# Weight splits of the output products, a first norm and clearing moved, and weights placed 64 bytes further, in a two-block transformer kernel on one core

## The chip, the cores and the metric

The kernel runs on one core of a Trainium2 chip. Its metric is the device time of one execution in microseconds (us); the figure quoted is the median of three runs. The profile comes from one profiled execution. Engines are named as the profile names them: PE is TensorE (PEld its weight loads), DVE is VectorE, ACT is ScalarE, POOL is GpSimd, SP is SyncE, which issues the weight DMAs.

## The reference

The input is 256 tokens of width 1024. A first block runs one layer: a mixer (a gated delta rule over chunks on one half of the width, a gated linear recurrence on the other) and an MLP of width 4096 with a squared ReLU. A second block puts 16 learned tokens in front (272 tokens) and runs two layers, each of a gated MLP, a mixer (stick-breaking attention and a convolution, gated and joined) and another gated MLP:

```python
def second_block(...):
    h = jnp.concatenate([meta_b, x], axis=1)
    for l in range(DEPTH_2):
        h = h + 0.5 * swiglu(rmsnorm_2(h, ffn1_norm[l]), ...)
        h = h + hybrid_mixer(rmsnorm_2(h, mix_norm[l]), ...)
        h = h + 0.5 * swiglu(rmsnorm_2(h, ffn2_norm[l]), ...)
    h = rmsnorm_2(h, final_norm)
    return h[:, N_META:]

def hybrid_mixer(u, ...):
    q, k, v, a, b, g_sb, g_conv = jnp.split(u @ w_in, IN_SPLITS, axis=-1)
    y_sb = stick_breaking_attention(q, k, v) @ w_attn_out
    y_conv = conformer_conv(a, b, ...) @ w_conv_out
    m = jax.nn.sigmoid(g_sb) * y_sb + jax.nn.sigmoid(g_conv) * y_conv
    return m @ w_out
```

All is float32, with weights of some 243 MB that are read once.

## The kernel before, in words

Activations lie transposed, with the width on 128 partitions and tokens along the free axis. A product is a **job**: one tile of 128 output columns, accumulated in one PSUM bank over 2 to 32 k-tiles of 128. Each float32 operand is held as a high part and a rest, and a k-tile costs three matmuls: high weight by high x, high weight by low x, low weight by high x (the three matmul lines of `job`, L532, L533 and L534 in the profile). Their moving operand has 256 tokens, or 272 in the second block; in that block's second layer ("layer 2" in the title, `layer == 1` in the code) the 16 learned tokens are no longer needed after the attention's keys and values, and q, the two gates gc and gs, and everything behind them have 256.

`plan` lists the jobs in order, `layout` cuts them into **units** of up to 8 k-tiles (1024 weight columns) and packs units into chunks of 2048 columns, each one DMA on SP. For every unit ScalarE copies the raw weights to a high part `wh` (the copy on L274, five buffers) and VectorE subtracts it from the raw weights to get the rest `wl` (the subtraction on L286, four buffers). `POOLED` names the kinds whose every n-th split goes to GpSimd instead (L491): every fourth of the input products, every second of ys (attention output) and o2 (mixer output), every one of yc (convolution output), some of the first block. ys and yc have 4 k-tiles, so their units have 512 columns. `emit_split` issues splits up to `LEAD` = 3 units ahead of the product in work.

The order of instructions on each engine is fixed when the program is built. Work beside the products is written as generators, **flows**, that are stepped between the k-tiles of a job whenever a planner's clock for VectorE and TensorE says that they are due. On the chip each engine then takes its instructions strictly in that order. The planner prices instructions by formulas of its own; it knows nothing of the places of operands or of two engines being in each other's way.

The flows that matter here:
- `residual` adds a finished output tile to the stream `H`, makes the next product's operand (high part on ScalarE, low part on VectorE), and adds its squares to `acc1`. In the first block's mixer and in o2 the add of squares is on GpSimd (`add=pt`), else on VectorE.
- `norm_rows` sums `acc1` over partitions by small matmuls (`tok_sums`), takes the inverse root on VectorE with a dozen tiny instructions, and spreads it over partitions by matmuls again (`to_rows`, into `R`). The products don't wait for the norm, which is applied when they are evacuated; the first MLP applies it only at its end. But the small matmuls stand in TensorE's queue.
- `do_ys` multiplies the attention's gate by the ys tile; `do_yc` multiplies the other gate by the yc tile, adds both, and splits the sum into the operand of o2. The o2 products of the first two tiles are a `pair`: k-tiles 0 to 5 of both, then 6 and 7 of both.
- `layer_norm` makes the operand of yc.
- At the start of a mixer GpSimd clears buffers for queries and values (`QZ`, `VZ`), for the attention weights (`AM`) and some borders. They lie in an arena that takes the place of the MLP's hidden activations, so clearing waits for that MLP's last product.

In the built program the operands x start 128 bytes past a multiple of 256, and the weight buffers 192 bytes past one, 4096 bytes apart; a k-tile's weights are 512 bytes, a k-tile of x 1024 or 1280. In layer 2 q, gc and gs read x from token 16 on, 64 bytes further.

Of the kernel before, what the change touches and what calls it, by code (L numbers as in the profile page):

```python
# [15 lines left out]
NM = 16  # L16
# [6 lines left out]
MIX1 = 17100  # L23
MIX2 = 16200
XW = 320
LEAD = 3
MINLEAD = 2
RAW = 3
TMPS = 9
# [3 lines left out]
POOLED = [(("a", "b", "q", "k", "v", "gc", "gs"), 4), (("ys", "o2"), 2), (("yc", ), 1), (("o1b",), 2), (("K", "Q"), 8)]  # L33
# [73 lines left out]

def layout():
# [3 lines left out]
    for j, (_, _, _, _, _, kts) in enumerate(plan()):  # L112
        mine = []
        for ks in kts:
            n = 128 * len(ks)
            limit = 1024 if len(chunks) <= 2 else CHUNK_COLS
            if not chunks or chunks[-1][1] + n > limit:
# [106 lines left out]
def tile_hybrid_blocks(  # L224
# [11 lines left out]
    jobs = plan()  # L236

# [148 lines left out]
    def tick():  # L386
# [8 lines left out]
        while st["split"] < min(st["unit"] + LEAD + 1, len(units)) and clk["V"] < clk["P"] + AHEAD:  # L395
            emit_split(st["split"])
# [64 lines left out]
    for kinds, every in POOLED:  # L461
        mine = [i for i, u in enumerate(units) if jobs[u[0]][0] in kinds]
        on_pool.update(mine[every - 1::every])

    def emit_high(u):
        while st["high"] <= min(u, len(units) - 1):
            i = st["high"]
            _, ks, c, o = units[i]
            emit_dma(c)
            n = 128 * len(ks)  # L470
            h = whp.tile([128, 1024], F32R, tag="wh", name="wh")
# [3 lines left out]
            cp(h[:, 0:n], src)  # L475
# [5 lines left out]
    def emit_split(u):  # L481
        while st["split"] <= min(u, len(units) - 1):
            i = st["split"]
            emit_high(i + (i > 0))
            _, ks, c, o = units[i]
            n = 128 * len(ks)
            lo = wlp.tile([128, 1024], F32R, tag="wl", name="wl")
            was, cur[0] = cur[0], Flow()
            cur[0].t, cur[0].eng = h_at.pop(i), "A"
            if i in on_pool:  # L490
                nc.gpsimd.tensor_tensor(out=lo[:, 0:n], in0=raw[c][:, o:o + n], in1=wh[i][:, 0:n].bitcast(F32), op=SUB)  # L491
                op("G", 0.1 + 0.00215 * n)
            else:
                tt(lo[:, 0:n], raw[c][:, o:o + n], wh[i][:, 0:n].bitcast(F32), SUB)
# [4 lines left out]
            if i + 1 < len(units) and units[i + 1][2] != c:  # L499
# [6 lines left out]
    def job(kind, x, n, o=0, bank_=None, last=True, start=None):  # L506
# [14 lines left out]
        for u in mine:  # L521
            st["unit"] = u
            emit_split(u + MINLEAD)
            h, lo = wh.pop(u), wl.pop(u)
            clk["P"] = max(clk["P"], w_at.pop(u) + LAT)
            for i, k in enumerate(units[u][1]):
# [3 lines left out]
                s = slice(128 * i, 128 * i + 128)  # L530
# [419 lines left out]
    junk = const.tile([128, 128], F32, name="junk")  # L950
    zero = const.tile([1, 512], BF16, name="zero")
# [378 lines left out]
    start_flow(norm_rows(acc1[:, 0:T1], T1, 1.0 / 1024, 1e-6, R[:, 0:T1], [ev_sq2], ev_r2))  # L1330
# [86 lines left out]

    def swiglu(x, ev_r, o, n, next_g, old_phase, final=False):
# [28 lines left out]
        for m in range(FF2):  # L1447
# [5 lines left out]
            start_flow(evac(ga, ua, m))  # L1453
        x.done()
# [12 lines left out]
    def mixer(x, ev_r, layer, next_g, old_phase):  # L1467
# [9 lines left out]
        QZ = [arena.get(4, n) for _ in range(2)]  # L1477
# [3 lines left out]
        VZ = arena.get(3, 4, 192)  # L1481
# [24 lines left out]
        def keep_q(t, b, ev):  # L1506

            for i in range(2):
                p = slice(64 * i, 64 * i + 64)
                cp(QZ[i].f[p, t], b[p, 0:n])  # L1510
# [78 lines left out]
        def values():  # L1589
            yield from wait(ev_r, *ev_v)  # L1590
            for i, (s0, sn) in enumerate(sblocks):
# [4 lines left out]
                for par in range(2):  # L1596
                    p = slice(64 * par, 64 * par + 64)
                    act(VZ.f[0:sn, i, :, 128 * par:128 * par + 64], v4(b[0:sn])[:, :, p], AF.Copy, scale=RC[0:sn, i:i + 1])
# [14 lines left out]
        def head(hp, par):  # L1613
# [7 lines left out]
            for t0, tn in blocks:  # L1621
                S = t0 + tn
                mm(b[:, col:col + S], QZ[par].f[:, hp, t0 - o:t0 - o + 128], KT.f[:, hp, 0:S])
# [51 lines left out]
            V = VZ.f[:, :, hp, 64 * par:64 * par + 128]  # L1675
# [195 lines left out]
```

## Time and profile before

| | before |
|---|---|
| median of three runs | 1520.81 us (1519.14 to 1522.02) |
| profiled execution | 1520.58 us |
| its span, first to last instruction | 1518.9 us |
| PE / DVE / ACT / POOL busy, share of the span | 97% / 71% / 53% / 13% |
| granted TensorE clock, mean | 0.990 of full speed |
| HBM read | 245.63 MB |

A busy share says how much of the span an engine worked, not that it set the end. Matmuls are pipelined: each is listed with some 0.28 us, but they start about 0.12 us apart, and the distance of their starts is what a product costs. A bracket behind a row of a timeline gives how long the engine idled before it, and what ended that.

### The profile page before, as it was taken

To read this page: it belongs to the slowest core of one execution; us is meant where nothing else is said; L and a number is where in the kernel's file an instruction comes from. 1 tells how busy PE (TensorE), PEld (TensorE's weight loads), DVE (VectorE), ACT (ScalarE), POOL (GpSimd) and SP (SyncE) were. 2 spreads that over 40 slices of the span, in tenths; PEclk is the share of its full clock that TensorE was granted. 3 is DMA by queue.
4 is the path that set the end of the run, shared out by engine and by line. 5 is a ranking of instruction groups with operands and counts; after the bars stand their busy time and mean duration, and the time that the engine had idled before them with its cause. 6 is when DMAs were issued, how large, how long until landed. Compare 5 with 4: busy or idle time off the path is not lost.

```text
span 1518.9 us, 29471 instructions
## 1 busy us (share of the span) xinstructions
PE 1478.2 (97%) x12130; PEld 1457.5 (96%) x12130; DVE 1075.8 (71%) x1882; ACT 802.7 (53%) x1365; POOL 198.3 (13%) x236
## 2 busy tenths in 40 slices
PE   7999999999999999999999999999999999999997
PEld 6889899999999999999999999999999989999997
DVE  5986866667666568998866655666568996866664
ACT  4568666544544445555644444544444655555553
POOL 3330300000000012234400000000003233500000
PEclk9999999999999999999999999999999999999999
DMA  6312455554545544433455544545454423465552
GB/s 226 142 57 84 142 194 194 193 196 143 217 167 178 177 173 143 153 123 111 162 200 171 184 169 162 203 169 181 166 182 166 167 102 122 170 219 195 188 179 79
DMA packets 36376, 248.58 MB, mean 164 GB/s; under 512 B 3984, under 2 KB 5264, under 8 KB 12304
## 3 DMA queue, kind: packets, MB, share of 16 engines
q1 hardware_dynamic: 35248, 245.50, 45.7%
q8 instruction: 95, 1.56, 0.4%
q10 hardware_dynamic: 992, 1.19, 0.2%
q14 instruction: 41, 0.34, 0.1%
HBM read 245.63 MB, written 1.05 MB: 162 GB/s over the span
## 4 chain that ended last, share of the span: by engine, by line
PE 83%; DVE 12%; ACT 3%; issue 1%; POOL 1%; DMA 0%; DVEq 0%; SPq 0%; ACTq 0%; POOLq 0%
PE bank L532 26%; PE bank L534 26%; PE bank L533 26%; PE bank L317 4%; DVE bank L297 2%; DVE wl L286 2%; DVE arena L286 2%; DVE arena L297 2%; ACT arena L274 1%; DVE arena L313 1%; PE bank L321 1%; DVE x L286 1%; ACT wh L274 1%; DVE tmp L286 0%; POOL acc L309 0%
## 5 line engine op out<-in xcount | busy, mean ns | idle before, releaser
L532 PE MATMUL bank<-x,wh 128*128 128x272 f32 (+1 forms) x2752 | 796.1, 289 | 10.8 <-ACT x L274 9.8
L534 PE MATMUL bank<-x,wl 128*128 128x272 f32 (+1 forms) x2752 | 784.1, 285 | 5.6 <-DVE wl L286 4.7
L533 PE MATMUL bank<-x,wh 128*128 128x272 f32 (+1 forms) x2752 | 785.1, 285 | 3.0 <-DVE x L286 2.3
L286 DVE TENSOR_TENSOR wl<-raw,wh 128x1024 fp32r<-128x1024 f32 (+4 forms) x453 | 532.6, 1177 | 183.4 <-PE bank L534 152.6
L274 ACT ACTIVATE wh<-raw 128x1024 fp32r<-128x1024 f32 (+4 forms) x510 | 494.5, 976 | 257.0 <-issue 136.1
L532 PEld LDWEIGHTS bank<-x,wh 128*128 128x128 f32 x2752 | 523.8, 190 | 14.4 <-ACT x L274 10.9
L533 PEld LDWEIGHTS bank<-x,wh 128*128 128x128 f32 x2752 | 523.9, 190 | 6.3 <-DVE x L286 4.4
L534 PEld LDWEIGHTS bank<-x,wl 128*128 128x128 f32 x2752 | 523.5, 190 | 6.7 <-DVE wl L286 5.6
L534 PE MATMUL bank<-hid,wl 128*128 128x272 f32 (+1 forms) x960 | 270.6, 282 | 0.0
L533 PE MATMUL bank<-hid,wh 128*128 128x272 f32 (+1 forms) x960 | 270.6, 282 | 0.0
L532 PE MATMUL bank<-hid,wh 128*128 128x272 f32 (+1 forms) x960 | 270.6, 282 | 0.0
L533 PEld LDWEIGHTS bank<-hid,wh 128*128 128x128 f32 x960 | 180.6, 188 | 0.0
L532 PEld LDWEIGHTS bank<-hid,wh 128*128 128x128 f32 x960 | 180.6, 188 | 0.0
L534 PEld LDWEIGHTS bank<-hid,wl 128*128 128x128 f32 x960 | 180.6, 188 | 0.0
L491 POOL TENSOR_TENSOR wl<-raw,wh 128x512 fp32r<-128x512 f32 (+3 forms) x57 | 107.9, 1904 | 190.1 <-PE bank L534 90.9
L286 DVE TENSOR_TENSOR tmp<-bank,R 128x272 f32<-128x272 f32 (+1 forms) x184 | 78.7, 429 | 64.8 <-PE bank L534 63.9
L274 ACT ACTIVATE tmp<-tmp 128x272 f32<-128x272 f32 (+1 forms) x140 | 59.3, 425 | 114.6 <-DVE tmp L286 78.4
L297 DVE SCALAR_TENSOR_TENSOR bank<-arena,C,bank 128x272 f32<-128x272 f32 (+1 forms) x232 | 102.2, 490 | 3.7 <-ACT bank L274 2.5
L1484 POOL MEMSET arena<- 64x1088 f32 (+1 forms) x4 | 3.9, 976 | 761.9 <-PE bank L534 761.9
L286 DVE TENSOR_TENSOR hid<-tmp,hid 128x272 fp32r<-128x272 f32 (+1 forms) x120 | 51.7, 433 | 38.3 <-ACT hid L274 38.3
L274 ACT ACTIVATE hid<-tmp 128x272 fp32r<-128x272 f32 (+1 forms) x120 | 51.0, 426 | 42.3 <-DVE tmp L286 40.7
L274 ACT ACTIVATE x<-H,C 128x272 fp32r<-128x272 f32 (+2 forms) x64 | 30.0, 486 | 81.6 <-DVE H L286 81.2
(200 smaller groups left out, 949.8 us busy)
## 6 DMA issues: line engine op xcount, KB each, us to landing
raw<-in_w_dram SPq DMA_DIRECT2D x187, 1024.0 KB, 4.8
raw<-in_w_dram SPq DMA_DIRECT2D x32, 960.0 KB, 4.7
raw<-in_w_dram SPq DMA_DIRECT2D x16, 896.0 KB, 4.6
raw<-in_w_dram SPq DMA_DIRECT2D x2, 512.0 KB, 6.0
H<-in_xt_dram SPq DMA_DIRECT2D x1, 544.0 KB, 6.6
LG<-in_lgw_dram SPq DMA_DIRECT2D x1, 512.0 KB, 6.0
out_dram<-H SPq DMA_DIRECT2D x2, 256.0 KB, 2.2
LM<-in_cm_dram SPq DMA_DIRECT2D x1, 320.0 KB, 5.2
```

The costliest lines, as they stand in the source:

```text
L274: nc.scalar.activation(out, in_, func, scale=scale, **kw)
L286: nc.vector.tensor_tensor(out=out, in0=a, in1=b, op=fn)
L297: nc.vector.scalar_tensor_tensor(out=out, in0=a, scalar=s, in1=b, op0=op0, op1=op1)
L313: nc.vector.tensor_tensor_scan(out=out, data0=a, data1=b, initial=initial, op0=op0, op1=op1)
L317: nc.tensor.matmul(out, lhsT, rhs, start=start, stop=stop)
L321: nc.tensor.transpose(out, in_, identity)
L491: nc.gpsimd.tensor_tensor(out=lo[:, 0:n], in0=raw[c][:, o:o + n], in1=wh[i][:, 0:n].bitcast(F32), op=SUB)
L532: nc.tensor.matmul(acc, h[:, s], xh, start=first and done == 0, stop=False)
L533: nc.tensor.matmul(acc, h[:, s], xl, start=False, stop=False)
L534: nc.tensor.matmul(acc, lo[:, s], xh, start=False, stop=last and done == total - 1)
L1484: nc.gpsimd.memset(QZ[i].f[64 * (1 - i):64 * (1 - i) + 64], 0.0)
```

## The change

- **Loads.** ys and yc tiles are taken in twos: two units of 512 columns are one **load**, one copy on ScalarE and one split of 1024 columns. All other units are a load each; `LEAD` and the buffers count loads. Number and order of matmuls and DMAs stay.
- **Where splits run.** ys and o2 leave `POOLED`: all their splits are on VectorE. Of yc every second load stays on GpSimd. The add of squares behind o2 moves from GpSimd to VectorE.
- **First norm.** The flow `norm_rows` in front of the first MLP starts after its fifth tile (m = 4) and no longer ahead of the first.
- **Clearing once.** `QZ` and `VZ` get a buffer of their own, cleared by GpSimd once, in the first gated MLP of the second block (at m = 8). `AM` and the borders are cleared at each mixer as before.
- **64 bytes.** `wh` and `wl` buffers grow from 1024 to 1088 columns (4352 bytes apart). For q, gc and gs of layer 2 the weights are written and read 16 columns, 64 bytes, further on. The arenas and two small tiles are moved to make room.

```diff
-MIX1 = 17100
-MIX2 = 16200
+MIX1 = 16448
+MIX2 = 11800
+SHARED = ("ys", "yc")
+WBUF = 1024 + 64
+LATE = ("q", "gc", "gs")
-POOLED = [(("a", "b", "q", "k", "v", "gc", "gs"), 4), (("ys", "o2"), 2), (("yc", ), 1), (("o1b",), 2), (("K", "Q"), 8)]
+POOLED = [(("a", "b", "q", "k", "v", "gc", "gs"), 4), (("yc",), 2), (("o1b",), 2), (("K", "Q"), 8)]
...
+    loads, load_of = [], []
+    for u, (j, ks, c, o) in enumerate(units):
+        if jobs[j][0] in SHARED and nth_of_kind(j) % 2:
+            loads[-1][2] += 128 * len(ks)
+            load_of.append((len(loads) - 1, 128 * len(ks)))
+        else:
+            loads.append([c, o, 128 * len(ks), jobs[j][0], NM * (jobs[j][2] == 1 and jobs[j][0] in LATE)])
+            load_of.append((len(loads) - 1, loads[-1][4]))
...
-            h = whp.tile([128, 1024], F32R, tag="wh", name="wh")
+            h = whp.tile([128, WBUF], F32R, tag="wh", name="wh")
...
-            cp(h[:, 0:n], src)
+            cp(h[:, a:a + n], src)
...
-                s = slice(128 * i, 128 * i + 128)
+                s = slice(o_w + 128 * i, o_w + 128 * i + 128)
...
-    start_flow(norm_rows(acc1[:, 0:T1], T1, 1.0 / 1024, 1e-6, R[:, 0:T1], [ev_sq2], ev_r2))
...
     for m in range(FF1):
         start_flow(do_ff1(pairs["ff1"].pop(0) if m < 2 and "ff1" in PAIRED else job("ff1", xb, T1), m))
+        if m == 4:
+            start_flow(norm_rows(acc1[:, 0:T1], T1, 1.0 / 1024, 1e-6, R[:, 0:T1], [ev_sq2], ev_r2))
...
+    held_pool = ctx.enter_context(tc.tile_pool(name="held", bufs=1))
+    QZ = [held_pool.tile([128, 4, T2], F32, name=f"qz{i}") for i in range(2)]
+    VZ = held_pool.tile([128, 3, 4, 192], F32, name="vz")
...
+            if m == 8 and not zeroed:
+                zeroed.append(True)
+                zeros()
...
-        for i in range(2):
-            nc.gpsimd.memset(QZ[i].f[64 * (1 - i):64 * (1 - i) + 64], 0.0)
-            nc.gpsimd.memset(AM[i].f, 0.0)
-        nc.gpsimd.memset(VZ.f, 0.0)
+        for a in AM:
+            nc.gpsimd.memset(a.f, 0.0)
...
-            start_flow(residual(b, m, nx, next_g(m), acc1[:, 0:n], ev_sq, o, add=pt))
+            start_flow(residual(b, m, nx, next_g(m), acc1[:, 0:n], ev_sq, o))
```

## Rows read from the trace of the kernel before

**Rows 1.** The page's part 1: busy us, share of the span, instructions.
```profile
PE 1478.2 (97%) x12130; PEld 1457.5 (96%) x12130; DVE 1075.8 (71%) x1882; ACT 802.7 (53%) x1365; POOL 198.3 (13%) x236
```
**Rows 2.** Windows: stretch, its length, busy us (instructions) by engine, clock, DMA.
```profile
192.00:355.00 163.00, 163.00 (x1441) 163.00 (x1440) 108.62 (x175) 93.55 (x155) 0.00 (x0) 1.00 0.53 189
376.00:553.70 177.70, 177.70 (x1443) 177.70 (x1442) 110.48 (x156) 85.15 (x117) 0.00 (x0) 1.00 0.52 182
```
**Rows 3.** PE timeline at the start of the first MLP.
```profile
178.56 0.28 PE L532 MATMUL bank<-x,wh 128*128 128x256 f32 x1
...
181.97 1.01 PE L317 MATMUL bank<-ones,acc 128*128 128x1 f32 x4 [2.58 <-POOL acc L309]
...
188.65 0.91 PE L317 MATMUL bank<-M,nr 128*128 128x128 f32 x6
...
191.98 0.28 PE L532 MATMUL bank<-x,wh 128*128 128x256 f32 x1
```
**Rows 4.** Windows: the stretch behind that wait, clock third from the end.
```profile
182.60:190.00 7.40, 7.40 (x39) 7.27 (x40) 6.46 (x20) 2.90 (x7) 0.11 (x1) 0.60 0.42 146
```
**Rows 5.** DVE timeline there: the weights of tile m = 2.
```profile
178.44 1.23 DVE L286 TENSOR_TENSOR wl<-raw,wh 128x1024 fp32r<-128x1024 f32 x1 [0.47 <-ACT wh L274]
```
**Rows 6.** Windows: the o2 pairs of both layers, and what follows in layer 2.
```profile
719.10:732.10 13.00, 11.24 (x74) 10.61 (x74) 11.10 (x18) 6.70 (x11) 6.28 (x4) 0.87 0.42 144
...
1298.70:1309.00 10.30, 8.11 (x51) 7.39 (x50) 8.08 (x17) 5.84 (x11) 3.72 (x3) 0.83 0.47 177
...
1308.40:1326.00 17.60, 17.60 (x150) 17.60 (x151) 15.72 (x19) 10.79 (x22) 12.82 (x9) 1.00 0.55 196
```
**Rows 7.** PE timeline: waits in the output products of both layers.
```profile
722.43 0.39 PE L532 MATMUL bank<-x,wh 128*128 128x272 f32 x1 [1.38 <-ACT x L274]
...
1284.17 0.39 PE L534 MATMUL bank<-x,wl 128*128 128x256 f32 x1 [0.90 <-POOL wl L491]
...
1301.93 0.38 PE L532 MATMUL bank<-x,wh 128*128 128x256 f32 x1 [1.38 <-ACT x L274]
```
**Rows 8.** DVE timeline in the output products of layer 2.
```profile
1299.56 1.86 DVE L286 TENSOR_TENSOR arena<-arena 128x256 f32<-128x256 f32 x1
...
1301.79 0.42 DVE L286 TENSOR_TENSOR arena<-arena 128x256 f32<-128x256 f32 x1
...
1308.88 2.68 DVE L286 TENSOR_TENSOR wl<-raw,wh 128x1024 fp32r<-128x1024 f32 x1 [0.65 <-ACT wh L274]
```
**Rows 9.** POOL timeline in the same stretch.
```profile
1282.84 13.74 POOL L491 TENSOR_TENSOR wl<-raw,wh 128x512 fp32r<-128x512 f32 x10 [5.30 <-PE bank L533]
1299.32 1.83 POOL L491 TENSOR_TENSOR wl<-raw,wh 128x768 fp32r<-128x768 f32 x1 [2.73 <-PE bank L534]
...
1307.85 5.99 POOL L491 TENSOR_TENSOR wl<-raw,wh 128x1024 fp32r<-128x1024 f32 x2 [2.88 <-PE bank L534]
```
**Rows 10.** PE timeline: a gs product of layer 2, two starts 24 matmuls apart.
```profile
1265.08 0.28 PE L532 MATMUL bank<-x,wh 128*128 128x256 f32 x1
...
1267.96 0.28 PE L532 MATMUL bank<-x,wh 128*128 128x256 f32 x1
```
**Rows 11.** Windows: the gate products of layer 2.
```profile
1206.00:1252.00 46.00, 44.48 (x341) 42.16 (x339) 44.89 (x92) 26.25 (x63) 14.11 (x24) 1.00 0.34 120
1252.60:1275.60 23.00, 23.00 (x181) 22.36 (x180) 16.22 (x42) 11.18 (x26) 5.11 (x5) 1.00 0.32 116
```
**Rows 12.** POOL timeline at the start of layer 2's mixer.
```profile
1141.90 0.95 POOL L1484 MEMSET arena<- 64x1024 f32 x1 [390.37 <-PE bank L534]
...
1146.58 2.39 POOL L491 TENSOR_TENSOR wl<-raw,wh 128x1024 fp32r<-128x1024 f32 x1
```
**Rows 13.** DVE timeline there.
```profile
1143.34 0.50 DVE L297 SCALAR_TENSOR_TENSOR x<-H,C,x 128x272 fp32r<-128x272 f32 x1 [0.59 <-ACT x L274]
...
1146.65 2.35 DVE L293 TENSOR_SCALAR rs_y<-RC 128x3 int32<-128x3 int32 x1
```
**Rows 14.** PE timeline there.
```profile
1150.89 0.81 PE L317 MATMUL bank<-M,RC 16*128 16x16 f32 x4 [1.39 <-DVE RC L297]
```

More of the change, by code (lines that the diff above doesn't have):

```diff
@@ L105, in plan, with nth_of_kind @@
     return jobs
+def nth_of_kind(j):
+    jobs = plan()
+    n = 0
+    while n < j and jobs[j - n - 1][0] == jobs[j][0]:
+        n += 1
+    return n
 def layout():
@@ L111, in layout @@
     off = 0
-    for j, (_, _, _, _, _, kts) in enumerate(plan()):
+    for j, (kind, _, _, _, _, kts) in enumerate(plan()):
         mine = []
@@ L116, in layout @@
             limit = 1024 if len(chunks) <= 2 else CHUNK_COLS
-            if not chunks or chunks[-1][1] + n > limit:
+            both = 2 * n if kind in SHARED and nth_of_kind(j) % 2 == 0 else n
+            if not chunks or chunks[-1][1] + both > limit:
                 if chunks:
@@ L394, in tick @@
                     flows.sort(key=lambda f: f.rank)
-        while st["split"] < min(st["unit"] + LEAD + 1, len(units)) and clk["V"] < clk["P"] + AHEAD:
+        while st["split"] < min(load_of[st["unit"]][0] + LEAD + 1, len(loads)) and clk["V"] < clk["P"] + AHEAD:
             emit_split(st["split"])
@@ L461, in tile_hybrid_blocks @@
     for kinds, every in POOLED:
-        mine = [i for i, u in enumerate(units) if jobs[u[0]][0] in kinds]
+        mine = [i for i, load in enumerate(loads) if load[3] in kinds]
         on_pool.update(mine[every - 1::every])
     def emit_high(u):
-        while st["high"] <= min(u, len(units) - 1):
+        while st["high"] <= min(u, len(loads) - 1):
             i = st["high"]
-            _, ks, c, o = units[i]
+            c, o, n, _, a = loads[i]
             emit_dma(c)
-            n = 128 * len(ks)
-            h = whp.tile([128, 1024], F32R, tag="wh", name="wh")
+            h = whp.tile([128, WBUF], F32R, tag="wh", name="wh")
             src = raw[c][:, o:o + n]
@@ L481, in emit_split @@
     def emit_split(u):
-        while st["split"] <= min(u, len(units) - 1):
+        while st["split"] <= min(u, len(loads) - 1):
             i = st["split"]
             emit_high(i + (i > 0))
-            _, ks, c, o = units[i]
-            n = 128 * len(ks)
-            lo = wlp.tile([128, 1024], F32R, tag="wl", name="wl")
+            c, o, n, _, a = loads[i]
+            lo = wlp.tile([128, WBUF], F32R, tag="wl", name="wl")
             was, cur[0] = cur[0], Flow()
@@ L498, in emit_split @@
             st["split"] += 1
-            if i + 1 < len(units) and units[i + 1][2] != c:
+            if i + 1 < len(loads) and loads[i + 1][0] != c:
                 raw.pop(c)
@@ L949, in tile_hybrid_blocks @@
     gd = {}
-    junk = const.tile([128, 128], F32, name="junk")
-    zero = const.tile([1, 512], BF16, name="zero")
+    junk = pool1.tile([128, 128], F32, name="junk")
+    zero = pool1.tile([1, 512], BF16, name="zero")
     nc.gpsimd.memset(zero, 0.0)
@@ L1415, in tile_hybrid_blocks, with zeros @@
     ff1_phase = phase
+    ff1_phase.close()
+    held_pool = ctx.enter_context(tc.tile_pool(name="held", bufs=1))
+    QZ = [held_pool.tile([128, 4, T2], F32, name=f"qz{i}") for i in range(2)]
+    VZ = held_pool.tile([128, 3, 4, 192], F32, name="vz")
+    zeroed = []
+    def zeros():
+        for i in range(2):
+            nc.gpsimd.memset(QZ[i][64 * (1 - i):64 * (1 - i) + 64], 0.0)
+        nc.gpsimd.memset(VZ, 0.0)
     def swiglu(x, ev_r, o, n, next_g, old_phase, final=False):
@@ L1674, in head @@
             py = pairs[hp][0]
[L1675 removed]
+            V = VZ[:, :, hp, 64 * par:64 * par + 128]
             e = n - 256
```

19 lines of the change are left out of this document (9 added, 10 removed).

## The prediction

> **What bounds the kernel now.** I read the page's first part, then windows over long stretches, then every place where TensorE stands still, and for each the timelines of the engines that it waits for. TensorE is busy 97% of the span [rows 1], so time is to be had only where its matmuls start further apart than they must, or not at all. The stretches without small matmuls show how far apart they must start: 1441 matmuls of 256 tokens in 163.0 us are 113.1 ns each, 1443 of 272 tokens in 177.7 us 123.2 ns [rows 2]. Against these two distances I measure each place that the change touches.
>
> **First norm.** The fourth unit of the first MLP starts at 178.56 and the seventh at 191.98 [rows 3]. Between lie 6 + 24 + 24 matmuls, at 113.1 ns 6.1 us; the stretch takes 13.4, so 7.3 us are lost. [...] After the change the sum stands three tiles later, some 8 us, when the squares are long there. The small matmuls remain. The sum took 1.01 with the wait's own tail, the spreading 0.91 [rows 3]; I take 1.4 for both, between 1.0 and 1.9. Next in line is the split of tile m = 2's weights: it ends at 178.44 + 1.23 = 179.67 [rows 5], and the tile's third matmul, which reads it, would be due at 178.56 + 8 × 0.113 = 179.46. That is a wait of some 0.3. The flow's tiny VectorE instructions only move. Gain 7.3 − 1.4 − 0.3 = **5.6 us**, between 4.5 and 6.5.
>
> **ys, yc and o2.** The o2 pair of layer 1 takes 13.0 us for 74 matmuls, which is 9.1 at 123.2 ns: 3.9 lost. Layer 2's takes 10.3 for 51, 5.8 at 113.1: 4.5 lost, clock 0.83 [rows 6]. Behind it 150 matmuls take 17.6 us, 117.3 ns each, at the full granted clock [rows 6]: a second, slower rhythm, which came with the return of the clock; by 4.2 ns these are 0.6 more. A ys tile waits 0.90 for a GpSimd split [rows 7]. In all 9.9 us are there to be had.
>
> The pairs wait for their operand [rows 7], the end of `do_yc` on VectorE. There the same addition of two SBUF tiles takes 0.42 us or 1.86, and a split that elsewhere takes 1.23 takes 2.68 [rows 5, 8]; at both long ones GpSimd has a split under way, which began just before and ends with them [rows 9]. So a GpSimd split holds up VectorE's instructions with two SBUF operands until it ends. In layer 2's yc stretch ten such splits run back to back for 13.74 us [rows 9].
>
> After the change two splits of 1024 columns are left on GpSimd for each layer, 2.39 each [rows 12], and one of them falls before yc. VectorE's own work while yc runs is 8 × 3 × 0.42 = 10.1 for `do_yc`, plus 2048 columns of o2 weights at 1.23 per 1024, 2.5, plus one hold-up of about 1: 13.6 us. Products give it 32 × 3 × 0.113 = 10.9 for yc and 36 × 0.113 = 4.1 until k-tiles 6 and 7 are wanted, 15.0. It just fits; I leave 0.6 of waiting in each layer, by the steps that hop to ScalarE and back, and with so short a wait no slow clock and no second rhythm. In layer 1 the operand of yc comes late already, and the last GpSimd split would begin when yc does and hold it up: 1.0 more. Gain 9.9 − 2.2 = **7.7 us**. The ends are 0, where VectorE, with all splits and the adds of squares, becomes the bound itself, and 9.9.
>
> **64 bytes.** A gs product of layer 2 needs 1267.96 − 1265.08 = 2.88 us for 24 matmuls, 120.0 ns each [rows 10], though the clock is full and nothing waits; 6.9 more than any 256-token product that reads x from its start. Weights and x lie then at the same place modulo 256 bytes; the change puts them 64 bytes apart again, as in all other products. There are 20 such tiles, 480 matmuls, so 0 to 3.3 us. But from 1206 to 1252 VectorE is busy 44.89 of 46.0 us, and TensorE is not quite [rows 11]: there the products wait for VectorE somewhere, and quicker ones wait longer. Free of that are the tiles behind 1252.6, about six, 144 matmuls or 1.0 us, and half of the four q tiles, 0.3. Gain **1.3 us**.
>
> [...]
>
> **Clearing once.** At the mixer's start in layer 2 clearing begins at 1141.90, and the first pooled split follows at 1146.58 [rows 12]; there it holds up the norm's second tiny instruction, 2.35 us, and TensorE waits 1.39 for the norm [rows 13, 14]. Layer 1 shows the same once more. With `QZ` and `VZ` gone, some 0.8 us of clearing remain, and the split, whose operand is ready, begins at about 1142.7 and ends at 1145.1. The norm is then free, but the split lies over the low part of the mixer operand's last k-tile, 0.50 from 1143.34 [rows 13]. It comes at 1145.6, and the first product wants it with its 23rd matmul: it starts just before clearing could, at 1141.6, and 22 × 0.1232 later is 1144.3. A wait of 1.4 takes the place of one of 1.39. In layer 1, where the same reckoning gives 1.7, **0.3 us** are lost in all. Bounds: 2.8 gained (both waits gone), 3 lost. The single clearing itself lies in a stretch where GpSimd has nothing to do (POOL 0.00 in 376 to 553.7 [rows 2]).
>
> **The sum.** 5.6 + 7.7 + 1.3 − 0.3 = 14.3 us off the profiled execution's 1520.58, which lies 0.2 under the median shown: **1506.3 us**, 0.9% faster.
>
> **Rivals.**
> [...]
> 2. VectorE becomes the bound behind ys. Its work there grows by ys and o2 splits and eight adds; if what it gains by GpSimd's silence is eaten up, the second term is nil: 1514.0. For it: it is already busy 15.72 of 17.6 us in o2 [rows 6]. Against: that holds stretched instructions like the 2.68.
> 3. Slower: the second rhythm becomes the usual one, since all weight buffers now lie 4352 instead of 4096 bytes apart. It costs 4.2 ns a matmul [rows 2, 6]; of 12,130 [rows 1], 3,400 eat up the sum, and all would give 1506 + 51 = 1557. Against: k-tiles of x and of weights step by 1024 or 1280 and 512 bytes, so that their distance already runs through multiples of 256, at one steady distance of starts [rows 2]; 4352 is such a multiple.
> 4. It does not do what it says: the wait of the first norm moves behind a late split, or a planner thrown out of step loses as much elsewhere: within 3 us of 1520.
>
> **How the numbers follow.** My forecast has a chance of 0.50, rival 1 0.18, rival 2 0.20, rival 3 0.05, rival 4 0.07. The range: the best of all terms, 6.5 + 9.9 + 3.3 + 2.8, gives 1498, which needs all at once; I cut it to 1500. Above, rival 2 with the bad ends of first norm and clearing gives 1514 + 1.1 + 2.7 = 1518; beyond lie rivals 3 and 4. So 1500 to 1518. A difference of 0.2%, 3 us, is about what a measurement of this kernel tells from no change. Faster by more: 0.50 + 0.18 + 0.17 of rival 2 + 0.03 of rival 4 = 0.88; the same 0.07; slower 0.05.
>
> **What would show it.** First norm: no wait of TensorE for GpSimd's acc and a granted clock near 1 in the first MLP; its first seven tiles in about 21 us. Output products: no long `do_yc` additions, the pairs at 0.6 us of waiting, 113 ns behind them. The 64 bytes: gs starts 113 ns apart, and longer waits for VectorE before 1252. Clearing: the norm's tiny instructions short, a wait for x near the 23rd matmul of each mixer. I am wrong if VectorE has no idle time from ys on, or if long stretches show 117 ns.

## The result

The changed kernel takes 1511.12 us (median of four runs, 1510.12 to 1512.98) against 1521.41 beside it: a ratio of 0.994, interval 0.9917 to 0.9964. Twelve more runs of it on another chip have a median of 1512.81 against 1519.56, ratio 0.9953 (0.9935 to 0.9971). Of the times in this document one is left out, an execution of the variant mixer_splits_vector that took 1639.41 us at a granted clock of 0.84 where its other nine had 0.98 to 0.99. The profiled execution takes 1510.12 us, its span 1508.4: 10.5 less than before, where the prediction took off 14.3.

The page's part 1 of the kernel after: GpSimd's share has gone from 13% to 9%, VectorE's has not moved, although it took over the splits of ys and o2.

```profile
PE 1471.4 (98%) x12130; PEld 1451.6 (96%) x12130; DVE 1073.8 (71%) x1910; ACT 800.6 (53%) x1349; POOL 136.7 (9%) x189
```

I measured each stage on TensorE, from the start of its first product to that of the next stage's first, in both profiles. The difference, after less before, in us:

| stage | after − before |
|---|---|
| first block's mixer and its output product | +1.4 |
| first MLP, first seven units / the rest | −6.8 / +1.9 |
| a and b products, layer 1 / layer 2 | −0.2 / −0.3 |
| layer 1: g / ys / yc / o2 / first units of the next MLP | −1.8 / +4.8 / +1.1 / −4.1 / −0.4 |
| layer 2: q, k, v / gc / gs | 0.0 / −0.2 / −0.5 |
| layer 2: ys / yc / o2 / first units of the next MLP | −1.3 / 0.0 / −4.2 / −0.7 |
| from the last MLP's last unit to the end | +0.7 |

All other stages agree within 0.02 us. In layer 1 the −1.8 of g and 1.8 of the +4.8 of ys are the same eight small matmuls, which stand among ys products now and stood among g products before (g is short for gc and gs). Part by part that is 4.9 us from the first norm (−6.8 + 1.9), 0.5 from layer 1's output products and 6.2 from layer 2's, 0.7 from the 64 bytes, 0.5 from clearing, less 1.4 at the beginning and 0.7 at the end. In these two stretches the change moves nothing but places: the weight buffers lie elsewhere, and at the beginning the arena and two small tiles.

**Where the gains came.** TensorE's timeline after, first MLP: the starts of the fourth and the seventh unit, 54 matmuls apart as in [rows 3], then the norm's sum and its spreading, which stand later.

```profile
180.19 0.28 PE L552 MATMUL bank<-x,wh 128*128 128x256 f32 x1
...
186.55 0.28 PE L552 MATMUL bank<-x,wh 128*128 128x256 f32 x1
...
190.09 0.50 PE L338 MATMUL bank<-ones,acc 128*128 128x1 f32 x4
...
194.65 1.02 PE L338 MATMUL bank<-M,nr 128*128 128x128 f32 x6 [0.20 <-DVE nr L318]
```

The stretch takes 6.36 us instead of 13.4; the wait for GpSimd is gone, and a wait of 0.20 for VectorE has come. Windows of the kernel after, in this order: the same norm with a clock of 1.00 where it was 0.60 [rows 4], a long stretch of 256 and one of 272 tokens, both o2 pairs, what follows in layer 2, and the gates.

```profile
189.00:196.50 7.50, 7.30 (x61) 6.97 (x60) 6.98 (x21) 5.06 (x9) 0.11 (x1) 1.00 0.54 201
...
199.20:349.00 149.80, 149.80 (x1324) 149.80 (x1323) 100.61 (x162) 86.07 (x143) 0.00 (x0) 1.00 0.55 193
373.00:550.00 177.00, 177.00 (x1438) 177.00 (x1437) 110.04 (x154) 84.75 (x117) 0.00 (x0) 1.00 0.53 182
719.80:725.80 6.00, 6.00 (x51) 6.00 (x50) 4.69 (x10) 3.93 (x7) 0.00 (x0) 1.00 0.52 176
1292.60:1299.40 6.80, 5.72 (x50) 5.52 (x49) 5.57 (x12) 4.97 (x8) 0.00 (x0) 1.00 0.40 139
1299.40:1315.70 16.30, 16.30 (x146) 16.30 (x145) 14.36 (x28) 10.15 (x21) 0.00 (x0) 1.00 0.57 202
1201.60:1247.60 46.00, 43.86 (x341) 41.28 (x340) 44.89 (x92) 26.36 (x63) 14.30 (x24) 1.00 0.36 120
```

The long stretches stand at 113.1 and 123.1 ns as before [rows 2]. The pair of layer 1 has no loss left (6.00 us for 51 matmuls), that of layer 2 one of 1.1 (6.80 for 50); before they took 13.0 for 74 and 10.3 for 51 [rows 6]. What follows in layer 2 is 144 matmuls in 16.3 us, 113 ns each, where it was 117.3 (a window counts the matmuls that it cuts at its ends too). In the gates VectorE is busy 44.89 of 46.0 us, to the digit as before [rows 11].

**Where layer 1's gain went.** TensorE's timeline of layer 1 after: the mean, the sums and the broadcast of the layer norm that makes yc's operand, and yc's first matmul.

```profile
686.24 1.99 PE L338 MATMUL bank<-arena,mean 128*128 128x272 f32 x8
...
694.00 1.39 PE L338 MATMUL bank<-ones,tmp 128*128 128x1 f32 x12
...
700.62 1.03 PE L338 MATMUL bank<-M,nr 16*128 16x16 f32 x6
704.63 0.59 PE L552 MATMUL bank<-x,wh 128*128 128x272 f32 x1 [2.98 <-ACT x L295]
```

The broadcast stands behind the last ys product, so nothing is left to do while the operand is made: yc waits 2.98 us, and a window shows a clock of 0.51 behind it: 22 matmuls in 6 us, where the pair of layer 1 at a clock of 1.00 has 51.

```profile
704.60:710.60 6.00, 5.97 (x22) 5.22 (x23) 2.97 (x7) 3.95 (x8) 0.00 (x0) 0.51 0.42 161
```

VectorE's timeline there, and a row of GpSimd's: three splits of ys weights right ahead of the mean, and a tiny instruction of the norm, which takes 1.05 us and ends with a GpSimd split of yc weights (0.17 where no such split runs).

```profile
680.08 1.22 DVE L307 TENSOR_TENSOR wl<-raw,wh 128x1024 fp32r<-128x1024 f32 x1
683.40 1.22 DVE L307 TENSOR_TENSOR wl<-raw,wh 128x1024 fp32r<-128x1024 f32 x1
...
685.83 1.22 DVE L307 TENSOR_TENSOR wl<-raw,wh 128x1024 fp32r<-128x1024 f32 x1
...
695.63 1.05 DVE L314 TENSOR_SCALAR rs_y<-nr 128x3 int32<-128x3 int32 x1
```

```profile
693.56 3.09 POOL L510 TENSOR_TENSOR wl<-raw,wh 128x1024 fp32r<-128x1024 f32 x1 [19.27 <-ACT wh L295]
```

### The profile page after: what moved, and what is told of

It reads as the page before. It is cut to its first block, busy times and chain, and to the rows that moved or that the text cites. A ratio compares the mean times of both kernels' runs of the same rounds, so it can differ in the third digit from the quotient of the medians.

```text
span 1508.4 us, 29363 instructions
## 1 busy us (share of the span) xinstructions
PE 1471.4 (98%) x12130; PEld 1451.6 (96%) x12130; DVE 1073.8 (71%) x1910; ACT 800.6 (53%) x1349; POOL 136.7 (9%) x189
## 3 DMA queue, kind: packets, MB, share of 16 engines
HBM read 245.63 MB, written 1.05 MB: 164 GB/s over the span
## 5 line engine op out<-in xcount | busy, mean ns | idle before, releaser
L307 DVE TENSOR_TENSOR wl<-raw,wh 128x1024 fp32r<-128x1024 f32 (+3 forms) x467 | 546.6, 1172 | 182.7 <-PE bank L554 153.9
L552 PEld LDWEIGHTS bank<-x,wh 128*128 128x128 f32 x2752 | 521.5, 190 | 13.8 <-ACT x L295 10.5
L510 POOL TENSOR_TENSOR wl<-raw,wh 128x1024 fp32r<-128x1024 f32 (+1 forms) x27 | 64.2, 2380 | 185.2 <-ACT wh L295 106.6
L307 DVE TENSOR_TENSOR tmp<-tmp,bank 128x272 f32<-128x272 f32 (+1 forms) x88 | 38.0, 432 | 39.0 <-ACT tmp L295 39.0
```

The costliest lines, as they stand in the source:

```text
L307: nc.vector.tensor_tensor(out=out, in0=a, in1=b, op=fn)
L510: nc.gpsimd.tensor_tensor(out=lo[:, a:a + n], in0=raw[c][:, o:o + n], in1=wh[i][:, a:a + n].bitcast(F32), op=SUB)
L552: nc.tensor.matmul(acc, h[:, s], xh, start=first and done == 0, stop=False)
```

## The experiments

Each kernel is the changed one with one edit. Stages are read from its profile. Most stages that an edit does not reach repeat within 0.03 us from kernel to kernel, so a stage tells more than a time. Not all do: in the seven profiles whose edit changes nothing in layer 1 from g to o2 (the changed kernel's two, no_offset, norm_back, clear_back, rephase and places) that stretch takes 127.1 to 128.5 us, the difference lying in yc (14.8 to 16.3), and a long run of 256-token matmuls can take 6 us more (see again). Times in us, the ratio (with its 95% interval) against the kernel before on the same chip:

| kernel | median (lowest to highest, runs) | span | ratio |
|---|---|---|---|
| no_offset | 1515.71 (1510.13 to 1517.45, 10) | 1515.4 | 0.9934 (0.9913 to 0.9955) |
| norm_back | 1516.49 (1512.44 to 1520.30, 10) | 1518.6 | 0.9940 (0.9915 to 0.9965) |
| outputs_back | 1517.06 (1514.26 to 1527.19, 10) | 1514.4 | 0.9979 (0.9951 to 1.0008) |
| clear_back | 1513.73 (1508.38 to 1517.11, 6) | 1506.7 | 0.9932 (0.9900 to 0.9964) |
| again | 1512.81 (1508.45 to 1517.08, 12) | 1507.1 | 0.9953 (0.9935 to 0.9971) |
| rephase | 1515.83 (1508.46 to 1517.03, 12) | 1513.1 | 0.9961 (0.9941 to 0.9982) |
| ahead_by_tiles | 1514.98 (1509.75 to 1518.73, 10) | 1514.5 | 0.9954 (0.9931 to 0.9977) |
| ys_shared_out | 1514.21 (1509.69 to 1517.32, 10) | 1515.6 | 0.9963 (0.9946 to 0.9980) |
| low_parts_out | 1506.55 (1506.26 to 1507.93, 4) | 1504.5 | 0.9885 (0.9850 to 0.9920) |
| first_split_vector | 1508.31 (1504.48 to 1511.12, 4) | 1507.8 | 0.9893 (0.9854 to 0.9932) |
| places | 1517.20 (1514.70 to 1520.45, 10) | 1513.0 | 0.9958 (0.9936 to 0.9981) |
| mixer_splits_vector | 1522.92 (1518.33 to 1529.92, 9) | 1516.6 | 0.9994 (0.9965 to 1.0023) |

**no_offset**

```diff
-LATE = ("q", "gc", "gs")
+LATE = ()
```

> The changed kernel with the weights of layer 2's 256-token products back at the start of their buffers. Theory: the place of the weights sets the distance of starts. In the changed kernel the q and gs products start 113 ns apart, before the change 120; they go back to 120 here, and 1.0 us is lost (0.4 to 1.5), since what the change gained there was eaten up by waits for VectorE (q gained 0.55 us and the next k product waited 0.56 more). Rival A: the distance stays at 113, because it came from the other places of x and of the arena; no change of time. Rival B: the distance goes back to 120 and all 20 tiles pay in full, 480 matmuls by 6.9 ns, 3.3 us.

TensorE's timeline of a q product in layer 2, first matmul and the next product's first, 24 apart: without the 64 bytes, then in the changed kernel.

```profile
1170.41 0.28 PE L552 MATMUL bank<-x,wh 128*128 128x256 f32 x1
...
1173.28 0.29 PE L552 MATMUL bank<-x,wh 128*128 128x272 f32 x1
```

```profile
1164.01 0.28 PE L552 MATMUL bank<-x,wh 128*128 128x256 f32 x1
...
1166.74 0.29 PE L552 MATMUL bank<-x,wh 128*128 128x272 f32 x1
...
1183.66 0.49 PE L342 MATMUL bank<-M,arena 128*16 128x128 f32 x3 [0.57 <-DVE arena L307]
```

The product takes 2.87 against 2.73 us; away from the first matmuls the starts stand 120 against 113 ns apart. So the place of the weights sets the distance, and rival A is out. q, k and v together take the same time in both, since the changed kernel waits 0.57 us for VectorE in its last row here. gc and gs lose 0.7; the theory had 1.0 in all, between 0.4 and 1.5. Rival B's 3.3 are out too.

**places**

```diff
+PLACES = {u: 8 * ((u - 74) // 4 % 8) for u in range(74, 106)}
+PLACES.update({u: 8 * ((u - 115) // 4 % 8) for u in range(115, 176)})
...
-... NM * (jobs[j][2] == 1 and jobs[j][0] in LATE)])
+... PLACES.get(u, NM * (jobs[j][2] == 1 and jobs[j][0] in LATE))])
```

> The changed kernel with the weights of the second MLP product (256 tokens) and of the first gated MLP's up, gate and down products of layer 1 (272 tokens) moved inside their buffers by 0, 32, 64, ... 224 bytes, four tiles at each place. The weights lie 64 bytes behind the x operand modulo 256 at the first place, and at the same place as x at the seventh (192 bytes). Theory: only the same place is dear; ff2 starts 120 ns apart at the seventh place and 113 (or 117.7) at the seven others, so ff2 takes 0.7 us more. The 272-token products stay at 123.4 at all places, or get dearer at the seventh. Rival A: each place has a distance of its own, and some place is better than 113 or 123. Rival B: the place does nothing here, and the 120 ns of layer 2 came from x at its 64-byte offset together with weights at their old place.

Windows of the second MLP product (256 tokens), weights moved by 0, 32, 128 and 192 bytes, then of the gated MLP (272 tokens), moved by 0, 64 and 224.

```profile
262.50:273.10 10.60, 10.60 (x96) 10.60 (x95) 6.71 (x16) 6.82 (x19) 0.00 (x0) 1.00 0.57 199
273.60:284.60 11.00, 11.00 (x94) 11.00 (x93) 6.85 (x14) 5.46 (x11) 0.00 (x0) 1.00 0.56 192
...
308.00:319.00 11.00, 11.00 (x96) 11.00 (x95) 6.78 (x11) 5.11 (x8) 0.00 (x0) 1.00 0.54 192
...
330.70:341.50 10.80, 10.80 (x92) 10.80 (x92) 6.66 (x9) 4.90 (x7) 0.00 (x0) 1.00 0.54 194
...
377.50:388.50 11.00, 11.00 (x91) 11.00 (x91) 8.45 (x13) 7.16 (x10) 0.00 (x0) 1.00 0.72 270
...
401.50:412.80 11.30, 11.30 (x91) 11.30 (x90) 6.82 (x10) 5.01 (x8) 0.00 (x0) 1.00 0.53 175
...
462.00:473.00 11.00, 11.00 (x90) 11.00 (x89) 6.65 (x10) 4.94 (x7) 0.00 (x0) 1.00 0.49 174
```

A window cut at both ends counts a matmul more or less, so I take the distances from the single starts: at 256 tokens 113.3, 120, 118.7, 120, 117.7, 118, 120 and 118.3 ns for 0, 32, ... 224 bytes; at 272 tokens 123.4, 123.4, 126.7, 126.7, 126.7, 125.7, 125.3 and 125.4. The theory falls, since not only the common place is dear: 32 and 96 bytes have 120 ns too. Of rival A the first half holds, several places with distances of their own; no place beats the one that the kernel has had all along, 64 bytes behind x. At 272 tokens the weights run through the places a second time, with the same distances. At 256 they do so once, and the values of 117.7 to 118.7 may be the slower rhythm of 117.7 ns that other kernels show at the old place (see again); this run does not part the two. ff2 takes 3.8 us more, the gated MLP 2.9.

**norm_back** starts `norm_rows` ahead of the first MLP again.

```diff
-        if m == 4:
-            start_flow(norm_rows(acc1[:, 0:T1], ...))
...
+    start_flow(norm_rows(acc1[:, 0:T1], ...))
     phase = ExitStack()
```

> The changed kernel with the first norm started ahead of the first MLP again. Theory: the whole gain of that stretch hangs on this one move; the first seven tiles of the MLP take 20.9 us again instead of 14.1 and the rest 1.9 less, so 4.9 us are lost, 1515.0, with the wait for GpSimd's last add of squares (2.58 before) and a granted clock near 0.6 behind it. Rival: the wait is back, but without the slow clock behind it, 2.6 us lost, 1512.7. Second rival: 0.9 us of mix1 and 0.5 of the o1 products, which got longer in the changed kernel, are a price of the move; they come back too, and only 3.5 are lost.

TensorE's timeline, and the window behind it:

```profile
181.97 1.02 PE L338 MATMUL bank<-ones,acc 128*128 128x1 f32 x4 [2.58 <-POOL acc L330]
...
188.70 0.91 PE L338 MATMUL bank<-M,nr 128*128 128x128 f32 x6
```

```profile
182.50:190.00 7.50, 7.50 (x40) 7.37 (x39) 6.47 (x20) 2.86 (x7) 0.11 (x1) 0.59 0.41 144
```

Wait and slow clock are those of [rows 3, 4], so the first rival is out. The first seven units take 21.2 us against 14.1, 7.0 lost. Less the 1.9 that the norm costs at its later place (from the table of stages; the rest of the MLP runs at 117.7 ns in this profile) that is 5.1; the theory had 4.9. The first mixer and its output, 168.1 us in the changed kernel, take 166.7 here, as before the change and as the second rival had it. But rephase, places and mixer_splits_vector keep the move and take 165.3 to 165.8, and the others, whose edits do not reach this stretch either, up to 169.1. So it is no price of the move, and the second rival is out too.

**outputs_back**

```diff
-SHARED = ("ys", "yc")
+SHARED = ()
...
-POOLED = [(..., 4), (("yc",), 2), (("o1b",), 2), (("K", "Q"), 8)]
+POOLED = [(..., 4), (("ys", "o2"), 2), (("yc", ), 1), (("o1b",), 2), (("K", "Q"), 8)]
...
-            start_flow(residual(b, m, nx, next_g(m), acc1[:, 0:n], ev_sq, o))
+            start_flow(residual(b, m, nx, next_g(m), acc1[:, 0:n], ev_sq, o, add=pt))
```

> The changed kernel with the third part undone: one tile to a buffer in ys and yc, half of the ys and o2 splits, all yc splits and o2's adds of squares on GpSimd again. Theory: the part gained what it was to gain at the o2 pairs (4.1 and 3.5 us) and at the ys waits and the rhythm of o2 in layer 2 (2.7), and lost 4.0 us in layer 1 at ys and yc, because VectorE has 2.5 us more of splits ahead of the layer norm's chain there: undone, 6.7 us are lost in all, 1516.8, and ys with yc in layer 1 take 28.5 us again instead of 34.3 (1.8 of it the mean's matmuls, which move back into the g products). Rival: the 4.0 us of layer 1 come from another part (clearing, or the place of the buffers); then ys and yc stay at 34 us and 10.7 are lost, 1520.8.

Layer 2 loses all of its 6.2 us again. In layer 1 ys and yc take 29.9 us instead of the changed kernel's 34.3, o2 25.9 instead of 23.7, g 71.3 instead of 69.5; in sum 127.1 against 127.1 to 128.5. The span is 6.0 longer. So in layer 1 the part moves a loss from o2 to ys and yc and gains nothing. That yc and ys come down shows that their loss belongs to this part, and the rival is out.

**ahead_by_tiles, ys_shared_out, low_parts_out, mixer_splits_vector** ask what fixes layer 1. Their edits:

```diff
# ahead_by_tiles
-        while st["split"] < min(load_of[st["unit"]][0] + LEAD + 1, len(loads)) and ...
+        while st["split"] < load_of[min(st["unit"] + LEAD, len(units) - 1)][0] + 1 and ...
-            emit_split(i + MINLEAD)
+            emit_split(load_of[min(u + MINLEAD, len(units) - 1)][0])
# ys_shared_out
-POOLED = [(..., 4), (("yc",), 2), (("o1b",), 2), (("K", "Q"), 8)]
+POOLED = [(..., 4), (("ys", "yc"), 2), (("o1b",), 2), (("K", "Q"), 8)]
# low_parts_out
+            left_out = loads[i][3] in SHARED and OUT0 <= i < OUT1 and i not in on_pool
-            lo = wlp.tile([128, WBUF], F32R, tag="wl", name="wl")
+            lo = wh[i] if left_out else wlp.tile([128, WBUF], F32R, tag="wl", name="wl")
# mixer_splits_vector
-POOLED = [(..., 4), (("yc",), 2), (("o1b",), 2), (("K", "Q"), 8)]
+POOLED = [(("o1b",), 2), (("K", "Q"), 8)]
```

> The changed kernel, with the splits running ahead by three tiles again, not by three buffers, which hold six tiles of ys or yc. Theory: layer 1 loses 4.0 us at ys and yc because VectorE makes splits for ys and yc before the last additions of the convolution, which the mean's matmuls wait for: the mean starts 2.2 us later, against TensorE, than before the change, and the broadcast of the norm stands behind the last ys product, so that yc waits 2.98 us. With fewer splits ahead the norm's chain comes 1.2 us or more earlier and the broadcast moves in between ys products: ys and yc of layer 1 take 29 to 32 us instead of 34.3, 2 to 5 us gained. Rival A: only the number of splits on VectorE counts, not when they are made; at most 0.5 us. Rival B: GpSimd's yc split, which holds up rs_y for 1.05 us, is the cause; no change.

> The changed kernel with every second ys buffer split on GpSimd too (two of four in each layer, 2.4 us each). Theory: the 2.5 us of splits that VectorE took over ahead of the norm's chain are what makes layer 1's yc late; ys and yc of layer 1 take 29 to 32 us instead of 34.3. In layer 2 GpSimd's split holds up VectorE or comes late for TensorE as before the change, 0 to 1.3 us lost at ys. In all 1 to 4 us gained. Rival (hold-up by GpSimd is the cause): ys and yc of layer 1 stay at 34 us or get longer.

> The changed kernel without VectorE's six splits of ys and yc weights in layer 1, 1.22 us each (the high part stands in for the low one, so the output differs). The stretch from layer 1's first g product to its last o2 product takes 126.8 to 127.5 us in five kernels that wait at quite different places in it. Theory: VectorE's work sets that length; without 7.3 us of it the stretch takes 121 to 123 us, 4.5 to 6.5 gained. Rival: the chain of the layer norm with its hops over ScalarE and the order of TensorE's queue set it; 126 us or more, and yc still waits about 3 us for ScalarE.

> The changed kernel with no GpSimd split at all in layer 2's two mixers: the nine of 1024 columns of each mixer's a to gs weights and the two of its yc weights go to VectorE, 1.22 us each there. Theory: a GpSimd split of 2.4 us stops VectorE's instructions with two SBUF operands until it ends, so it costs VectorE about what it saves; a and b gain 1.1 in each mixer as with the first split alone, the g products of layer 1 and gc with gs of layer 2, where VectorE is busy over 90%, stay within 1 us of 69.45 and 68.9, and the whole is 1 to 4 us faster than the changed kernel. Rival: VectorE pays 1.22 us for each split and gets little back; g and gc with gs get 3 to 5 us longer each, layer 1's stretch to the last o2 product 4 to 7 us longer, and the kernel is slower than the changed one by 4 us or more.

Layer 1 from its first g product to its last o2 product; mean and broadcast are their starts, counted from that first g product:

| kernel | mean | broadcast | ys + yc | whole | VectorE busy |
|---|---|---|---|---|---|
| low_parts_out | 67.6 | 79.9 | 27.6 | 124.2 | 104.8 |
| before | 68.0 | 81.2 | 28.5 | 127.5 | 112.7 |
| ahead_by_tiles | 69.1 | 84.2 | 30.9 | 126.8 | 112.4 |
| changed | 70.2 | 84.6 | 34.3 | 127.5 | 110.9 |
| mixer_splits_vector | 79.7 | 87.8 | 40.9 | 132.4 | 111.3 |

Two of these wholes as windows show them, of low_parts_out and of mixer_splits_vector, and behind the second TensorE's waits in it.

```profile
614.86:739.05 124.19, 121.58 (x928) 116.18 (x927) 104.81 (x224) 71.50 (x153) 24.79 (x42) 1.00 0.37 131
```

```profile
612.31:744.71 132.40, 124.65 (x928) 119.89 (x927) 111.28 (x237) 71.87 (x153) 13.01 (x36) 0.95 0.36 123
```

```profile
PE bank L552 <- ACT x L295: 2.9, 1, 2.9
PE bank L338 <- DVE nr L318: 2.3, 1, 2.3
PE bank L338 <- DVE tmp L307: 2.2, 2, 1.9
```

ahead_by_tiles brings the mean 1.1 us forward and ys with yc down by 3.5, as expected, but the g products get back their small matmuls (+1.8), a ys tile waits 1.91 for its split, and of the whole 0.3 to 1.7 are left, by which of the changed kernel's 127.1 to 128.5 it is set against. ys_shared_out ends with 30.3 for ys and yc and 127.1 for the whole. In both the theory is right about the place and wrong about the gain. low_parts_out leaves out 7.3 us of splits and answers with 3.3 (2.9 to 4.3): less than the theory's 4.5 to 6.5, more than the rival's 1.5, and the rival's wait of yc for ScalarE is not there.

mixer_splits_vector splits the question. VectorE has six more splits in this stretch, 7.3 us, but is busy only 0.4 us longer, and 3.1 longer in layer 2 from gc to o2 (105.9 against 102.8): here a GpSimd split costs VectorE nearly all of what it saves, there over half, as the theory had it. Its conclusion fell all the same. The rival's size came true, 4.9 us longer here and 8.8 in layer 2 (122.6 against 113.8), but at another place than it named: the g products got 1.6 us shorter in layer 1 and 6.7 in layer 2, and ys with yc 6.6 and 16.4 longer. So VectorE's sum does not set ys and yc. What stands ahead of the norm's chain in its queue does: eight splits start from 669.42 to 691.45, where the changed kernel has four from 670.24 to 685.83, the mean starts 9.5 us later, and TensorE waits for the chain in the three rows above. In all five kernels ys with yc take the longer, the later the mean starts, and it starts the later, the more ys and yc columns VectorE splits ahead of it (none, 512, 1024, 3072 and 7168). The whole does not follow that order: before, ahead_by_tiles and changed differ by 0.7 us.

**clear_back**

```diff
-            if m == 8 and not zeroed:
-                zeroed.append(True)
-                zeros()
...
-        for a in AM:
-            nc.gpsimd.memset(a.f, 0.0)
+        for i in range(2):
+            nc.gpsimd.memset(QZ[i][64 * (1 - i):64 * (1 - i) + 64], 0.0)
+            nc.gpsimd.memset(AM[i].f, 0.0)
+        nc.gpsimd.memset(VZ, 0.0)
```

> The changed kernel with QZ and VZ cleared by GpSimd at each mixer's start again, in the tiles that are held now. Theory: one wait of TensorE at the mixer's start is exchanged for another; the a and b products take 26.8 us in both layers again instead of 26.57 and 26.49, 0.5 us lost, 1510.6. Rival: the clearing's 4 us on GpSimd cost more than the wait at the start because they push the pooled splits of the a and b products back; 2 us lost or more. Second rival: nothing there depends on clearing; within 0.2 us.

Theory and both rivals are wrong: a and b take 26.24 us in both layers, 0.3 less than with clearing once. At layer 2's start the changed kernel's GpSimd split begins 1.0 us behind the first product, holds up the operand's last low part, and the 23rd matmul waits; its timelines of GpSimd, VectorE and TensorE:

```profile
1138.55 2.38 POOL L510 TENSOR_TENSOR wl<-raw,wh 128x1024 fp32r<-128x1024 f32 x1
```

```profile
1139.23 2.00 DVE L318 SCALAR_TENSOR_TENSOR x<-H,C,x 128x272 fp32r<-128x272 f32 x1 [0.59 <-ACT x L295]
```

```profile
1141.29 0.39 PE L553 MATMUL bank<-x,wh 128*128 128x272 f32 x1 [0.89 <-DVE x L318]
```

In clear_back the split begins 4.0 us behind the first product and lies over the norm's tiny instruction instead, where TensorE waits 0.85:

```profile
1144.66 0.81 PE L338 MATMUL bank<-M,RC 16*128 16x16 f32 x4 [0.85 <-DVE RC L318]
```

Before the change the split began 5.0 us behind the first product and the same wait was 1.39 [rows 14]. With a buffer of its own one of the three clearings runs long before the mixer. That buffer helps, then; clearing once does not.

**first_split_vector**

```diff
+START = (179, 381)
...
+    on_pool -= {load_of[u][0] for u in START}
```

> The changed kernel with the first GpSimd split of each of layer 2's mixers (the one that begins at the mixer's start, while VectorE makes the operand's last low part) on VectorE instead. Theory: the waits of 1.0 and 0.9 us at the 23rd matmul are the price of that split's hold-up, which stretches a 0.50 us instruction to 2.00; without it the a and b products take 25.6 to 25.8 us in both layers instead of 26.57 and 26.49, 1.6 us gained. Rival: VectorE's own 1.22 us for the split stand in the same place and the norm's chain waits for them instead; 0.5 us or less gained.

VectorE's timeline at layer 2's start: the split, and behind it the low part, unstretched.

```profile
1137.90 1.22 DVE L308 TENSOR_TENSOR wl<-raw,wh 128x1024 fp32r<-128x1024 f32 x1
1139.04 0.50 DVE L319 SCALAR_TENSOR_TENSOR x<-H,C,x 128x272 fp32r<-128x272 f32 x1
```

a and b take 25.45 and 25.44 us, and TensorE waits nowhere in them: 2.2 us gained, more than expected. Of the versions that compute the whole this is the best found. Its ratio of 0.9893 stands below the changed kernel's, but its interval overlaps both of the changed kernel's; the 2.2 us rest on the stages.

**again** is the changed kernel unaltered; **rephase** adds three matmuls:

```diff
     for m in range(FF1):
+        if m == 9:
+            if len(free_banks) < 3:
+                force(lambda: len(free_banks) >= 3)
+            b = free_banks.pop(0)
+            h = wh[load_of[st["unit"] + 1][0]]
+            for i in range(3):
+                mm(b[:, 0:T2], h[:, 0:128], h[:, 0:T2], i == 0, i == 2)
+            give(b)
```

> The changed kernel itself once more, as the measure for its variants on this chip. In the profiles so far the long run of 1375 matmuls from the first norm's last small matmul to the second MLP's first interruption goes at 113 ns a matmul in some executions and at 117.7 in others, of one and the same program, and the ten times of the variant without the 64 bytes fall into two groups, 1510.1 to 1511.0 and 1514.9 to 1517.5. Theory: the changed kernel has the same two groups, near 1510 and 1516, and its four times at 1510 to 1513 were mostly of the faster one. Rival: the slower rhythm belongs to the variants; all times here lie between 1509 and 1513.

> The changed kernel with three matmuls of 272 tokens, whose result is not used, ahead of tile m = 9 of the first MLP (0.4 us of work). In the profiles each of the 15 q products with offset weights that follow a 272-token product settles at 113 ns, while behind small matmuls of the norms 45 runs settle at 113 and 19 at 117.7. Theory: a 272-token matmul ahead of the long run sets the 113 ns rhythm; ff1 behind it and ff2 take 87.0 in the profile, the times fall into one group near 1510.5 and the median is 2 to 4 us below that of the changed kernel run beside it. Rival: what follows is chance as after any interruption; two groups as before, 0.4 us higher.

Windows over the long run of 256-token matmuls: first again, then no_offset, whose instructions there are the same.

```profile
207.00:351.00 144.00, 144.00 (x1273) 144.00 (x1272) 95.39 (x154) 81.24 (x135) 0.00 (x0) 1.00 0.54 191
```

```profile
206.50:356.50 150.00, 150.00 (x1276) 150.00 (x1275) 95.54 (x155) 81.53 (x135) 0.00 (x0) 1.00 0.53 183
```

That is 113.1 against 117.6 ns, 6 us, at full clock with no wait. The same is seen in one and the same program: a part of a gs tile of layer 2, two starts 16 matmuls apart, first in the changed kernel's first profile, then in again.

```profile
1248.87 0.28 PE L554 MATMUL bank<-x,wl 128*128 128x256 f32 x1
...
1250.69 0.28 PE L552 MATMUL bank<-x,wh 128*128 128x256 f32 x1
```

```profile
1248.37 0.28 PE L554 MATMUL bank<-x,wl 128*128 128x256 f32 x1
...
1250.25 0.28 PE L552 MATMUL bank<-x,wh 128*128 128x256 f32 x1
```

That is 1.82 against 1.88 us, 114 against 117.5 ns. The changed kernel's twelve times run from 1508.5 to 1517.1, wider than its first four and than the rival allows, but in no two clear groups, so the theory's groups are not shown either. rephase failed: its profile shows 113 ns ahead of the three matmuls and 117.7 behind them, and its times scatter as widely.

## Why the prediction was right, and where not

The parts gave 12.8 us of the 14.3 forecast; the start and the end, which no term held, took 2.1 of them back. Every part has the sign that was forecast, but for clearing, and the mechanisms were the forecast's, but for layer 1's output products.

- **First norm, 5.6 forecast, 4.9 measured** (norm_back 5.1). The wait of 2.58 us and the clock of 0.60 behind it [rows 3, 4] are gone: TensorE waits for no add of squares there, and the clock is 1.00. The small matmuls cost 1.9 instead of 1.4, and the seven units ran in the slower rhythm, 120 matmuls by 4.4 ns, 0.5 us; the 0.3 us of waiting for the split of tile m = 2 did not come. In no_offset, where these units run at 113 ns, it did: that tile takes 0.4 us longer than the next, by a wait for VectorE at its third matmul.
- **ys, yc, o2, 7.7 forecast, 6.7 measured: the step that failed is layer 1's share.** Of 9.9 − 2.2, layer 1's part was 3.9 − 0.6 − 1.0 = 2.3, and it gave 0.5 (between 0.9 and −0.6 by the seven profiles named above); layer 2's was 5.4 and gave 6.2. "VectorE's own work while yc runs" was the wrong stretch to count. The pair's loss of layer 1 is gone as forecast. But ys splits, which ran on GpSimd in part, now stand on VectorE ahead of the layer norm's chain, in twos and so up to six tiles early. The mean starts 2.2 us later, the broadcast 3.4, and it misses the ys products, so yc waits 2.98 us and runs on at a clock of 0.51. The forecast's 1.0 for a GpSimd split at yc's start named that place for another reason.
- **64 bytes, 1.3 forecast, 0.7 measured.** 113 ns as said, and part of the gain swallowed by waits for VectorE as said. The q tiles, 0.3 forecast, gave nothing, since their 0.5 went into the wait of 0.57; gc and gs gave 0.7 of 1.0, and some of their tiles stand at 118 ns. That the 64 bytes do nothing, to which 0.18 went as rival 1, is out: in no_offset and places, products that differ in the place of the weights alone stand 113 to 120 ns apart.
- **Clearing, 0.3 loss forecast, 0.5 gain measured.** The exchange of one wait for another was right, at the matmul named; the waits are 1.0 and 0.9 where 1.7 and 1.4 were reckoned, so the sign came out the other way. By clear_back the gain comes from the buffer of its own: 1.1 us in the two layers with clearing at each mixer, of which clearing once takes 0.6 back.
- **Rival 2** came half true: in layer 1 alone, and by the order of VectorE's work, not by its sum. **Rival 3's** slower rhythm exists, but comes and goes in one and the same program; long stretches of the profile after stand at 113.1.
- The start's 1.4 us and the end's 0.7 are not shown to be effects of the change: in again, the same program, the end takes 0.8 less. Its start is the changed kernel's, but norm_back, with the same places, has the start of the kernel before.

What stays open is what sets layer 1's whole at 127 to 128 us in kernels with such different waits: low_parts_out gets 3.3 of 7.3 us back, so splits are a part of it, not all. Open too is what chooses the rhythm at an interruption.

## What to carry to other kernels

Moving work from a hindering engine to a busy one is counted up to the next chain that the busy engine must deliver, not only where the stall stood: ask what is now ahead of that chain in its queue. Doubling a buffer doubles how far ahead a lookahead counted in buffers runs. Where one GpSimd instruction lies over VectorE's critical one, move that one; moving one in each layer gained 2.2 us, moving all of them lengthened the stretches from g to o2 by 4.9 and 8.8.

## What the runs showed of the hardware

- In no_offset and places the place of the weights against the moving operand, moved there within 256 bytes, went with the distance of starts: 113 or 120 ns at 256 tokens (with values near 118 between, which may be the other rhythm), 123.4 to 126.7 at 272.
- At one place a run of 256-token matmuls goes at 113 or at 117.7 ns: again and no_offset differ by 6 us in one run of some 1300, 113.1 against 117.6 ns. In rephase the distance went from 113 to 117.7 at the three matmuls put in between. The changed kernel's times spread over 8.6 us; that the rhythm makes up most of that is likely but not shown, since in both its profiles the long run stands at 113.
- GpSimd's splits hold VectorE up: six splits more on VectorE lengthen its busy time by 0.4 us in layer 1 and 3.1 in layer 2 instead of 7.3. In the profile before, all 27 of its instructions on 256 or 272 columns without an operand in PSUM that begin under a split, 0.2 us or more ahead of its end, end 0.28 to 0.30 us behind it; the 63 with an operand in PSUM take 0.41 to 0.51, as elsewhere. A norm instruction of three elements a partition, with one operand in its row, was held too: in the profile after it took 1.05 us instead of 0.17 and ended at 696.68, where the split ends at 696.65.
- The engines took their instructions in the order of the built program: in the trace of the kernel before, all 11,136 matmuls with `wh` or `wl` and ScalarE's 1346 activations stand in that order, by the shapes of their rows.
